# Seven-product feed-forward groups: products copied and accumulated in PSUM, two fewer VectorE combinations, and another order of loads and steps

## The chip, the core and the metric

The kernel runs on one core of a Trainium2 chip. Its time is the device time of one execution in microseconds (us); several executions give a median. One further execution is recorded by the hardware profiler, and its rows are the trace that this document reads.

## The reference

Two layers of an encoder on 256 tokens of width 1024, all in float32. A layer is a feed-forward part, attention, and a second feed-forward part; only the feed-forward parts are touched here.

```
D_MODEL = 1024; SEQ = 256; DEPTH = 2; D_FF = 2816
def swiglu(h, w_gate, w_up, w_down):
    return (jax.nn.silu(h @ w_gate) * (h @ w_up)) @ w_down
for l in range(DEPTH):
    x = x + 0.5 * swiglu(rms_norm(x, ffn1_norm[l]), ffn1_w_gate[l], ffn1_w_up[l], ffn1_w_down[l])
    x = x + attention(rms_norm(x, mix_norm[l]))     # windowed and differential heads, w_in, w_out
    x = x + 0.5 * swiglu(rms_norm(x, ffn2_norm[l]), ffn2_w_gate[l], ffn2_w_up[l], ffn2_w_down[l])
return rms_norm(x, final_norm)
```

## The kernel before

**Precision.** TensorE multiplies in a reduced float format, fp32r. Each float32 operand is split into a high part (a ScalarE copy to fp32r, in the trace a CAST) and a low part (VectorE: operand minus high part). A product is three matmuls: high by high, low by high, high by low.

**Weights.** All weights come in pieces of 1 MB, 128 partitions by 4 by 512 float32, listed in `specs` in the order of use. SP loads a piece into one of six buffers (`raw`, `N_RAW = 6`). Each piece is split in two halves of 128 x 1024; a half becomes a high and a low tile from a pool of 28 (`s4`). A buffer is free for the next load when the second half of what it holds has been split. `ahead` interleaves three streams in program order, each as far ahead of use as it may go: loads (`dma`, up to `AHEAD = 10` steps ahead, as long as a buffer is free), preparations (`prep`) and splits (`split`, up to `look` half pieces ahead of the half in use). ScalarE, VectorE and GpSimd keep the written order in the feed-forward parts (`Kept`), TensorE always.

**A feed-forward part.** The 2816 columns are five groups of 512 and one of 256. The products for gate and up of a group, then SiLU and product (`h`, 256 tokens by 512), are followed by the down product of the group before it, in two halves of 512 output columns (`down(g, 0)`, `down(g, 1)`), which accumulate over all groups in four PSUM banks (`accs`). `h` is turned by TensorE (`turn`: eight 128x128 transposes, then a high copy on ScalarE and a low part on VectorE).

**Seven products.** Groups 2 to 4 of the first feed-forward part and groups 1 to 4 of the other three (`SEVEN`), 15 in all, compute gate and up together in the Strassen-Winograd form: of the two halves of the tokens (columns of the turned x) and the two halves of K there are seven products of 128x512x512 instead of eight. With a, d the upper and lower K half of gate and b, c those of up, the weights of the products are a, d, c, a+b, b+c, a+b+c and a+b+c+d. Each is formed in the raw buffers before it is split:

- b+c and a+b are formed by accumulating DMAs that GpSimd issues (`gather`: `pool.dma_start(raws[to], w[k], accum_op=ALU.add)`). The first is issued when b has landed (`behind=`); the second when a has been split (`prep` of the step behind a).
- a+b+c and a+b+c+d are formed by VectorE in the buffer of a (`plus`, two adds of 128x1024 each). So the buffer of a holds in turn a, a+b, a+b+c and a+b+c+d.

Order of the steps before: a, b+c, d, c, down half 0, a+b, a+b+c, a+b+c+d, down half 1. In the first seven-group that is group 1, b+c stands behind c. The x-side sums (`make_sums`) are made once for a part.

**PSUM.** Eight banks of 128 x 512 float32, all under the tag `ps`. In a seven-group the four combinations of products (u1, g1, u0 in two steps, ...) are formed on VectorE from PSUM and from copies that ScalarE makes (`m1`, `m7`).

Of the kernel before, what the change touches and what calls it, by code (L numbers as in the profile page):

```python
# [12 lines left out]
ALU = mybir.AluOpType  # L13
# [21 lines left out]
def trunk(ctx: ExitStack, tc: tile.TileContext, x, n1, g1, u1, d1, nm, w_in, sink,  # L35
# [35 lines left out]
    def bank():  # L71
        return ps.tile([P, 512], F32, tag="ps", bufs=8, name=nm_("ps"))

# [18 lines left out]
    class Step:  # L92
        def __init__(self, kn, n, moves, key=None, prep=None, src=None, free=None, behind=None):
            self.kn, self.n, self.moves, self.prep = kn, n, moves, prep
# [164 lines left out]
    for l in range(DEPTH):  # L259
        def ffn_specs(wg, wu, wd, sevens):  # L260
# [3 lines left out]
            for g in range(1, NGRP):  # L264
                downs = [down(g - 1, h) for h in range(2)]
                if g in sevens:
                    specs.extend(seven(wg[l], wu[l], g * 512, downs, g == 1))
                else:
                    specs.extend(plain(w[l], g * 512, 512, k0, 4) for w in (wg, wu) for k0 in (0, 4))
                    specs.extend(downs)  # L270
            for k0 in (0, 4):
# [34 lines left out]
    class Norm:  # L306
# [42 lines left out]
        def make_sums(self):  # L349
# [18 lines left out]

            s1 = add(b1, t1, ALU.subtract)
            s2 = add(s1, t0, ALU.add)  # L370
            yield
# [158 lines left out]
    def tokens(accs, xs, w, k0, ks=range(4), first=0, last=KC - 1, order=None, cols=slice(None), h=None):  # L530

        for k, t in (order or [(k, t) for k in ks for t in range(2)]):
            kk = k0 + k
            hi, lo = w.part(k, cols, h)
            xv = xs[kk // 2][:, kk % 2]
            xh, xl = xv[:, t * P:(t + 1) * P], xv[:, S + t * P:S + (t + 1) * P]
            pe.matmul(accs[t], lhsT=xh, rhs=hi, start=kk == first, stop=False)
# [22 lines left out]
    def first_groups(norm, ws):  # L560

        sls = [halves(bank()) for _ in ws]
        for k in range(0, KC, 2):
# [38 lines left out]
    def ffn(norm, aside=None, before=None, final=False, sevens=SEVEN[1]):  # L602
# [33 lines left out]

        def by_seven(h, g):


            flat = lambda: tmp().rearrange("p a n -> p (a n)")  # L640

            def put(o, x, y, op):
                dve.tensor_tensor(o, x, y, op=op)
                return o

            late, run = g == max(sevens), 1 in sevens
            m1, m7 = flat(), flat()


            if g > 1:  # L650
                g0 = prod(norm.quarter(0, 0), weights())
                act.copy(m1, g0)
                p7 = prod(norm.summed(3), weights(1, True))
                act.copy(m7, p7)
                hT = turn(h, 2)
                prod(norm.quarter(0, 1), weights(), g0)
                p3 = prod(norm.summed(2), weights())
                if not run:
                    g0 = silu(flat(), g0, 0)
                down(hT, g - 1, 0, weights())  # L660
                if run:
                    g0 = silu(flat(), g0, 0)
            else:
                p1 = prod(norm.quarter(0, 0), weights(1, True))
                hT = turn(h, (0,))
                w = weights(1, True)
                act.copy(m1, p1)
                p2 = prod(norm.quarter(0, 1), w)
                hT += turn(h, (1,))
                g0 = put(flat(), p2, m1, ALU.add)  # L670
                down(hT, 0, 0, weights())
                silu(g0, g0, 0)
                p3 = prod(norm.summed(2), weights())
                p7 = prod(norm.summed(3), weights(1, True))
                act.copy(m7, p7)
            h = blk(F32)
            p5 = prod(norm.summed(0), weights())
            prod(norm.summed(1), weights(look[0] - 5 if late else run, late or run), p7)
            u1 = put(m1, p7, m1, ALU.subtract)
            p4 = prod(norm.quarter(1, 1), weights(look[0] - 4 if late else 3 * run, late or run))  # L680
            g1 = put(flat(), p4, u1, ALU.subtract)
            w = weights(look[0] - 3 if late else 2 * run)
            silu(g1, g1, 1)
            put(u1, u1, p5, ALU.subtract)
            u0 = put(m7, u1, m7, ALU.subtract)
            put(u0, u0, p3, ALU.add)
            if run and g == max(sevens) - 1:
                ahead(2 * at["use"] - 2 + look[0] - 1)
            up(h, u0, g0, 0)
            up(h, u1, g1, 1)  # L690
            down(hT, g - 1, 1, w)
            return h
# [12 lines left out]

        accs = [[bank(), bank()] for _ in range(2)]

        def down(hT, g, h, w):
            tokens(accs[h], [None] * (2 * g) + hT, w, 4 * g, last=(FC - 1, G4 - 1) if final and h else FC - 1)


        gs, us = [bank(), bank()], [bank(), bank()]
        if before is None:
# [33 lines left out]
        for n in range(1, NGRP):  # L747
            if n in sevens:
                look[0] = IN_FFN + min(sevens) - n if before is not take_x else IN_MIX - (n == NGRP - 1)
                h = by_seven(h, n)  # L750
                continue
            sums = norm.make_sums()
            gs = [bank(), bank()]
            tokens(gs, norm.xs, weights(), 0)
            hT = turn(h, 2)
            norm.copies()
# [4 lines left out]
            us = [bank(), bank()]  # L761
# [4 lines left out]
            for hh in range(2):  # L766
                down(hT, n - 1, hh, weights())
                if hh == 0:
                    next(sums, None)

        gu = [bank(), bank()]
        tokens(gu, norm.xs, weights(), 0)
# [55 lines left out]
    def mix(l, norm, nxt_norm):  # L828
# [23 lines left out]

        def scores(q, kb, dist, slopes, init, den):

            sl = [bank(), bank()]
            for t in range(2):
# [19 lines left out]
        def soft_b(h, q):  # L876

            den = den_b[:, h]
            e, _ = scores(q, kbs["b", h], distB, [slopeB[h]] * 2, [3e38] * 4, den)
            d2 = den.rearrange("p (t a) -> p a t", a=2)  # L880
# [56 lines left out]
        vB = tp.tile([P, 2, 512], F32, tag="v", bufs=1, name=nm_("v"))  # L937
        vsl = [bank() for _ in range(2)]
        for k0 in (0, 4):
# [44 lines left out]
        oT = [blk() for _ in range(4)]  # L984
        rsl, osl = [[bank() for _ in range(2)] for _ in range(2)]
        for t in range(2):
# [175 lines left out]
```

## Time and profile before

| | |
|---|---|
| Median of 3 executions | 918.29 us (917.4 to 919.19) |
| Profiled execution | 917.39 us, its span 915.6 us |
| Matmul on TensorE (PE) | 904.5 us busy, 99% |
| VectorE (DVE) | 792.5 us, 87% |
| ScalarE (ACT) | 589.8 us, 64% |
| GpSimd (POOL) | 66.4 us, 7% |
| Granted TensorE clock | 0.999 |

A timeline row has the start, the length, the engine, the line of the kernel, the operation with what it writes and reads, its count, and in brackets how long the engine had been idle and what ended that. Nearly all rows name L50, the helper that issues for the kept engines, so groups are told apart by their tiles: `raw` weights, `w` split weights, `s` a tile of the `s4` pool (split x or h), `q` and `v` the x-side sums, `tmp` scratch, `ps` PSUM. A DMA's row on an engine is its issue; from issue to landing is given apart. "a <-b" names as releaser the last semaphore that the profile sees.

### The profile page before, as it was taken

To read this page: it belongs to the slowest core of one execution; us is meant where nothing else is said; L and a number is where in the kernel's file an instruction comes from. 1 tells how busy PE (TensorE), PEld (TensorE's weight loads), DVE (VectorE), ACT (ScalarE), POOL (GpSimd) and SP (SyncE) were. 2 spreads that over 40 slices of the span, in tenths; PEclk is the share of its full clock that TensorE was granted. 3 is DMA by queue.
4 is the path that set the end of the run, shared out by engine and by line. 5 is a ranking of instruction groups with operands and counts; after the bars stand their busy time and mean duration, and the time that the engine had idled before them with its cause. 6 is when DMAs were issued, how large, how long until landed. Compare 5 with 4: busy or idle time off the path is not lost.

```text
span 915.6 us, 12544 instructions
## 1 busy us (share of the span) xinstructions
PE 904.5 (99%) x4696; PEld 763.7 (83%) x4696; DVE 792.5 (87%) x1096; ACT 589.8 (64%) x917; POOL 66.4 (7%) x83
## 2 busy tenths in 40 slices
PE   8999999999999999999999999999999999999997
PEld 6888888899888888888888888888998888888886
DVE  6768999959975999999789999997797689999994
ACT  7836676557865766576486666665677496666561
POOL 0400100000010100100010010000001010010011
PEclk9999999999999999999999999999999999999999
DMA  9996898828436698898767998887463467998831
GB/s 339 355 238 173 265 297 268 238 93 240 136 108 189 158 280 248 257 273 275 258 164 201 276 285 217 265 293 219 116 230 98 139 153 201 275 289 230 259 132 47
DMA packets 114061, 200.87 MB, mean 219 GB/s; under 512 B 3662, under 2 KB 31376, under 8 KB 114000
## 3 DMA queue, kind: packets, MB, share of 16 engines
q1 hardware_dynamic: 96528, 166.74, 54.5%
q0 software_dynamic: 16096, 31.75, 19.3%
q10 hardware_dynamic: 1376, 1.57, 0.5%
q8 instruction: 37, 0.61, 0.3%
q14 instruction: 24, 0.20, 0.1%
HBM read 199.00 MB, written 1.05 MB: 218 GB/s over the span
## 4 chain that ended last, share of the span: by engine, by line
PE 98%; issue 1%; DMA 0%; ACT 0%; DVE 0%; POOLq 0%; POOL 0%; ACTq 0%
PE ps L50 98%; DMA xk<-in_x_dram 0%; ACT w L50 0%; DVE s L50 0%; DVE xk L50 0%; ACT tmp L50 0%; ACT L50 0%; POOLq L1157 0%; POOL rf L50 0%; ACTq L50 0%; DVE tot L50 0%; DVE tmp L50 0%
## 5 line engine op out<-in xcount | busy, mean ns | idle before, releaser
L50 PE MATMUL ps<-w,s 128*128 128x512 f32 (+1 forms) x2574 | 600.2, 391 | 0.5 <-ACT tmp L50 0.5
L50 PEld LDWEIGHTS ps<-w,s 128*128 128x128 f32 x2574 | 477.6, 188 | 100.3 <-ACT tmp L50 2.3
L50 DVE TENSOR_TENSOR w<-raw,w 128x1024 fp32r<-128x1024 f32 (+1 forms) x458 | 482.1, 1101 | 37.8 <-ACT w L50 36.6
L50 ACT CAST w<-raw 128x1024 fp32r<-128x1024 f32 (+1 forms) x458 | 409.8, 954 | 122.6 <-DVE raw L50 78.4
L50 PE MATMUL ps<-w,q 128*128 128x512 f32 x540 | 127.3, 389 | 0.0
L50 PEld LDWEIGHTS ps<-w,q 128*128 128x128 f32 x540 | 101.4, 188 | 21.0
L50 PE MATMUL ps<-s,w 128*128 128x256 f32 x672 | 83.1, 284 | 0.0
L50 PEld LDWEIGHTS ps<-s,w 128*128 128x128 f32 x672 | 81.5, 192 | 0.5
L50 POOL DMA_DIRECT2D raw<-in_ffn_w_up_dram x30 | 38.9, 1296 | 472.8 <-DVE w L50 240.8
L50 DVE TENSOR_TENSOR raw<-raw,raw 128x1024 f32<-128x1024 f32 x60 | 70.7, 1219 | 0.0
L50 ACT ACTIVATE s<-ps,gcol 128x256 fp32r<-128x256 f32 (+1 forms) x80 | 31.7, 480 | 43.7 <-PE ps L50 42.1
L50 ACT CAST s<-ps 128x512 fp32r<-128x512 f32 x44 | 24.3, 594 | 29.9 <-PE ps L50 29.9
L50 PE MATMUL ps<-w,v 128*128 128x512 f32 x180 | 43.3, 389 | 0.0
L50 ACT COPY tmp<-ps 128x512 f32<-128x512 f32 x34 | 19.9, 585 | 36.2 <-PE ps L50 34.0
L50 ACT ACTIVATE s<-s,negm 128x256 f32<-128x256 f32 x64 | 31.9, 500 | 14.8 <-DVE negm L50 14.8
L50 PE MATMUL ps<-ident,s 128*128 128x128 f32 x304 | 39.7, 273 | 0.0
L50 PEld LDWEIGHTS ps<-w,v 128*128 128x128 f32 x180 | 33.8, 188 | 7.0
L50 PEld LDWEIGHTS ps<-ident,s 128*128 128x128 f32 x304 | 35.1, 140 | 5.1 <-issue 0.8
L50 DVE TENSOR_TENSOR s<-ps,s 128x512 fp32r<-128x512 f32 x44 | 28.7, 686 | 9.1 <-ACT s L50 9.1
L50 DVE SCALAR_TENSOR_TENSOR s<-ps,gcol,s 128x256 fp32r<-128x256 f32 x48 | 20.3, 478 | 11.6 <-ACT s L50 11.5
L50 DVE TENSOR_TENSOR tmp<-ps,tmp 128x512 f32<-128x512 f32 x37 | 25.4, 686 | 2.7 <-PE ps L50 2.1
L50 DVE TENSOR_TENSOR xk<-xk,ps 128x512 f32<-128x512 f32 (+1 forms) x25 | 14.1, 598 | 14.9 <-PE ps L50 14.9
(106 smaller groups left out, 404.7 us busy)
## 6 DMA issues: line engine op xcount, KB each, us to landing
raw<-in_ffn_w_down_dram SPq DMA_DIRECT2D x44, 1024.0 KB, 8.9
raw<-in_ffn_w_gate_dram SPq DMA_DIRECT2D x39, 1024.0 KB, 6.4
raw<-in_ffn_w_up_dram SPq DMA_DIRECT2D x39, 1024.0 KB, 5.7
raw<-in_ffn_w_up_dram POOLq DMA_DIRECT2D x30, 1024.0 KB, 12.3
raw<-in_w_in_dram SPq DMA_DIRECT2D x14, 1024.0 KB, 6.1
raw<-in_ffn_w_gate_dram SPq DMA_DIRECT2D x8, 512.0 KB, 6.2
raw<-in_ffn_w_up_dram SPq DMA_DIRECT2D x8, 512.0 KB, 7.2
raw<-in_w_in_dram SPq DMA_DIRECT2D x8, 512.0 KB, 5.3
```

The costliest lines, as they stand in the source:

```text
L50: ins = issue(*a, **k)
```

## The change

What it does, in a seven-group:

- PSUM becomes six single banks and one pair of banks (`xy`). ScalarE writes the negated first product p1 into both banks of the pair; the products of c and of b+c accumulate onto these. The product p5 of a+b is copied by ScalarE into the bank of p1, where p4 (weights a+b+c+d) accumulates; the product of a+b+c accumulates on p5 itself. VectorE then needs three combinations, two fewer. The x-side sums change sign to fit.
- The add for a+b+c, and for a+b+c+d, is one VectorE instruction of 128x2048 instead of two of 128x1024.
- `h` is turned by token halves (`turn_one(h, t)`: four transposes, copy, low part, once for each half) instead of by column halves.
- Order of the steps: a, down half 1 deferred from the group before (`below`, of the h two groups back), d, c, down half 0, a+b, b+c, a+b+c, a+b+c+d. So b is loaded last, behind the down piece, and each down half 1 is used in the next group. In a first seven-group without an earlier one in its part it is a, d, down half 0, c, and then the same.
- The four accumulators are taken when first used, the look-ahead (`lead`) is 8, 8, 7, 7 half pieces instead of 8, 7, 6, 5 in parts with four such groups, and the preparation of a+b+c may go one step earlier (`early=1`).

The number of matmuls, of loads and of accumulating DMAs stays as it was. VectorE has 1098 instructions before and 1038 after, ScalarE 855 and 837, counted in the program.

```diff
-        return ps.tile([P, 512], F32, tag="ps", bufs=8, name=nm_("ps"))
+        return ps.tile([P, 512], F32, tag="ps", bufs=6, name=nm_("ps"))
+    def pair():
+        return ps.tile([P, 2, 512], F32, tag="xy", bufs=1, name=nm_("xy"))
...
-    def seven(wg, wu, c0, downs, first):
+    def seven(wg, wu, c0, below, down):
...
-                for h in (0, 2):
-                    x_, t_ = [raws[i][:, h:h + 2] for i in (x, to)]
-                    dve.tensor_tensor(t_, t_, x_, op=ALU.add)
+                dve.tensor_tensor(raws[to], raws[to], raws[x], op=ALU.add)
...
-        bc = Step(4, 512, load(b), key=b, behind=gather(c, b))
-        rest = [Step(4, 512, load(d), key=d, free=[]), Step(4, 512, load(c), key=c, free=[]), downs[0]]
-        steps = [rest[0], rest[2], rest[1], bc] if first else [bc] + rest
+        steps = [Step(4, 512, load(d), key=d, free=[]), Step(4, 512, load(c), key=c, free=[])]
+        steps = [below] + steps + [down] if below is not None else [steps[0], down, steps[1]]
         steps[0].prep = lambda: issue(gather(b, a), 1)
         return [Step(4, 512, load(a), key=a, free=[])] + steps + [
                 Step(4, 512, None, src=a, free=[]),
-                Step(4, 512, None, prep=plus(c, a), src=a, free=[c]),
-                Step(4, 512, None, prep=plus(d, a), src=a, free=[a, d]),
-                downs[1]]
+                Step(4, 512, load(b), key=b, behind=gather(c, b)),
+                Step(4, 512, None, prep=plus(c, a), src=a, free=[c], early=1),
+                Step(4, 512, None, prep=plus(d, a), src=a, free=[a, d])]
...
-                    (specs[at["prep"]].prep is None or at["split"] >= 2 * at["prep"]):
+                    (specs[at["prep"]].prep is None or at["split"] >= 2 * (at["prep"] - specs[at["prep"]].early)):
...
+        def turn_one(h, t):
+            sl = bank()
+            for k in range(4):
+                pe.transpose(sl[:, k * P:(k + 1) * P], h[:, t, k * P:(k + 1) * P], ident)
+            hb = blk()
+            act.copy(hb[:, 0], sl)
+            dve.tensor_tensor(hb[:, 1], sl, f(hb[:, 0]), op=ALU.subtract)
+            return hb
...
+        def by_sevens(h, groups, old):
...
+            xy = pair()
+            for g in groups:
+                start, late = old is None, g == groups[-1]
+                look[0] = lead(g)
+                p1 = prod(norm.quarter(0, 0), weights(start, start))
+                act.activation(xy, p1.unsqueeze(1).to_broadcast([P, 2, 512]), AF.Copy, scale=-1.0)
+                if start:
+                    g0 = flat()
+                    act.copy(g0, p1)
+                new = [turn_one(h, 0)]
+                if start:
+                    p2 = prod(norm.quarter(0, 1), weights())
+                    new.append(turn_one(h, 1))
+                    dve.tensor_tensor(g0, p2, g0, op=ALU.add)
+                    below(by_token(new), g - 1, 0, weights(), [(k, t) for t in range(2) for k in range(4)])
+                    silu(g0, g0, 0)
+                    prod(norm.summed(2), weights(), xy[:, 1])
+                else:
+                    below(old, g - 2, 1, weights())
+                    new.append(turn_one(h, 1))
+                    prod(norm.quarter(0, 1), weights(), p1)
+                    prod(norm.summed(2), weights(), xy[:, 1])
+                    below(by_token(new), g - 1, 0, weights())
+                    g0 = silu(flat(), p1, 0)
+                old = by_token(new)
+                p5 = prod(norm.summed(0), weights())
+                act.copy(p1, p5)
+                prod(norm.summed(3), weights(), xy[:, 0])
+                prod(norm.summed(1), weights(look[0] - 5 if late else 1, True), p5)
+                e = flat()
+                act.copy(e, p5)
+                u1, u0 = flat(), flat()
+                dve.tensor_tensor(u0, xy[:, 1], e, op=ALU.add)
+                dve.tensor_tensor(u1, xy[:, 0], e, op=ALU.add)
+                h = blk(F32)
+                up(h, u0, g0, 0)
+                p4 = prod(norm.quarter(1, 1), weights(look[0] - 4 if late else 3, True), p1)
+                g1 = flat()
+                dve.tensor_tensor(g1, p4, u1, op=ALU.subtract)
...
+                silu(g1, g1, 1)
+                up(h, u1, g1, 1)
+            below(old, groups[-1] - 1, 1, w)
             return h
...
-        accs = [[bank(), bank()] for _ in range(2)]
+        accs = []
+        def lead(n):
+            return IN_FFN - (n - min(sevens)) // 2 if before is not take_x else IN_MIX - (n == NGRP - 1)
```

The other edits take the pair of banks in place of two single ones in the plain groups and in the attention part, or fit callers to the new functions.

More of the change, by code (lines that the diff above doesn't have):

```diff
@@ L266, in ffn_specs @@
                 if g in sevens:
-                    specs.extend(seven(wg[l], wu[l], g * 512, downs, g == 1))
+                    specs.extend(seven(wg[l], wu[l], g * 512, down(g - 2, 1) if g > 1 else None, downs[0]))
+                    if g == max(sevens):
+                        specs.append(downs[1])
                 else:
                     specs.extend(plain(w[l], g * 512, 512, k0, 4) for w in (wg, wu) for k0 in (0, 4))
-                    specs.extend(downs)
+                    specs.extend(downs[:1] if g + 1 == min(sevens) else downs)
             for k0 in (0, 4):
@@ L560, in first_groups @@
     def first_groups(norm, ws):
-        sls = [halves(bank()) for _ in ws]
+        both = pair()
+        sls = [halves(both[:, i]) for i in range(2)]
         for k in range(0, KC, 2):
@@ L635, in prod @@
             return acc
-        def by_seven(h, g):
-            flat = lambda: tmp().rearrange("p a n -> p (a n)")
[L642 to L691, printed above, removed]
@@ new lines, in below @@
+        def below(of, g, h, w, order=None):
+            while len(accs) <= h:
+                accs.append([bank(), bank()])
+            tokens(accs[h], of, w, 4 * g, last=(FC - 1, G4 - 1) if final and h else FC - 1, order=order)
+        def by_sevens(h, groups, old):
+            flat = lambda: tmp().rearrange("p a n -> p (a n)")
+            xy = pair()
[15 more added lines that the diff above has]
+                    prod(norm.summed(2), weights(), xy[:, 1])
+                else:
+                    below(old, g - 2, 1, weights())
[19 more added lines that the diff above has]
+                dve.tensor_tensor(g1, p4, u1, op=ALU.subtract)
+                if late:
+                    w = weights(look[0] - 3)
+                else:
+                    ahead(2 * at["use"] + look[0] - 2)
+                silu(g1, g1, 1)
+                up(h, u1, g1, 1)
+            below(old, groups[-1] - 1, 1, w)
@@ L704, in turn, with both @@
             return out_
-        accs = [[bank(), bank()] for _ in range(2)]
+        accs = []
+        def lead(n):
+            return IN_FFN - (n - min(sevens)) // 2 if before is not take_x else IN_MIX - (n == NGRP - 1)
         def down(hT, g, h, w):
+            while len(accs) <= h:
+                accs.append([bank(), bank()])
             tokens(accs[h], [None] * (2 * g) + hT, w, 4 * g, last=(FC - 1, G4 - 1) if final and h else FC - 1)
-        gs, us = [bank(), bank()], [bank(), bank()]
+        def both():
+            p = pair()
+            return [p[:, t] for t in range(2)]
+        gs, us = [bank(), bank()], both()
         if before is None:
@@ L748, in ffn @@
             if n in sevens:
-                look[0] = IN_FFN + min(sevens) - n if before is not take_x else IN_MIX - (n == NGRP - 1)
-                h = by_seven(h, n)
+                if n == min(sevens):
+                    h = by_sevens(h, sevens, by_chunk(hT) if n > 1 else None)
                 continue
@@ L760, in ffn @@
             next(sums, None)
-            us = [bank(), bank()]
+            us = both()
             for k0 in (0, 4):
@@ L765, in ffn @@
             h = hidden(g, us)
-            for hh in range(2):
+            for hh in range(1 if n + 1 == min(sevens) else 2):
                 down(hT, n - 1, hh, weights())
@@ L851, in q_finish, with scores @@
             return [q[:, 0], q[:, 1]]
-        def scores(q, kb, dist, slopes, init, den):
-            sl = [bank(), bank()]
+        def scores(q, kb, dist, slopes, init, den, wide=False):
+            both = pair() if wide else None
+            sl = [both[:, i] if wide else bank() for i in range(2)]
             for t in range(2):
@@ L937, in mix @@
         vB = tp.tile([P, 2, 512], F32, tag="v", bufs=1, name=nm_("v"))
-        vsl = [bank() for _ in range(2)]
+        both = pair()
+        vsl = [both[:, t] for t in range(2)]
         for k0 in (0, 4):
@@ L984, in mix @@
         oT = [blk() for _ in range(4)]
-        rsl, osl = [[bank() for _ in range(2)] for _ in range(2)]
+        rsl, both = [bank() for _ in range(2)], pair()
+        osl = [both[:, t] for t in range(2)]
         for t in range(2):
```

24 lines of the change are left out of this document (15 added, 9 removed).

## The prediction

> **What bounds the kernel now.** I read the page's busy shares first, then the chain that ended last, then the costliest groups, and then the timelines of the engines over the first two seven-groups of the second FFN.
>
> ```profile
> span 915.6 us, 12544 instructions
> PE 904.5 (99%) x4696; PEld 763.7 (83%) x4696; DVE 792.5 (87%) x1096; ACT 589.8 (64%) x917; POOL 66.4 (7%) x83
> 31.04 873.94 PE ps L50 x4547
> ```
>
> The third line is one link of the chain of waits: from 31.04 us on the chain never leaves TensorE for 873.94 us. So a faster VectorE cannot shorten this run by itself; only fewer or denser matmuls could, and the change keeps all of them in number and shape. The question is whether TensorE stays fed.
>
> The pace of one seven-group stands in TensorE's timeline, by the transposes that open each group, and in the busy times of the stretches between:
>
> ```profile
> 343.59 1.03 PE L50 MATMUL ps<-ident,s 128*128 128x128 f32 x8
> ...
> 347.23 2.88 PE L50 MATMUL ps<-w,q 128*128 128x512 f32 x12
> 349.95 5.60 PE L50 MATMUL ps<-w,s 128*128 128x512 f32 x24
> ...
> 374.44 1.03 PE L50 MATMUL ps<-ident,s 128*128 128x128 f32 x8
> 405.25 1.04 PE L50 MATMUL ps<-ident,s 128*128 128x128 f32 x8
> 320.00:350.80 30.80, 30.80 (x141) 25.59 (x140) 29.59 (x31) 20.65 (x25) 2.57 (x2) 1.00 0.90 248
> ```
>
> A group lasts 30.8 us (405.25 - 374.44), and one product of 12 matmuls 2.72 (349.95 - 347.23). The last row is a stretch: start and end, length, then busy time of PE, PEld, DVE, ACT, POOL, then clock, DMA share, GB/s. VectorE is busy 29.6 of 30.8 us, so it is the second limit, close behind.
>
> **VectorE and ScalarE work.** The change drops two 128x512 combinations per group, 30 in all:
>
> ```profile
> L50 DVE TENSOR_TENSOR tmp<-tmp,ps 128x512 f32<-128x512 f32 x30 | 20.5, 684 | 0.5
> L50 DVE TENSOR_TENSOR raw<-raw,raw 128x1024 f32<-128x1024 f32 x60 | 70.7, 1219 | 0.0
> L50 ACT COPY tmp<-ps 128x512 f32<-128x512 f32 x34 | 19.9, 585 | 36.2 <-PE ps L50 34.0 <-DVE w L50 2.1
> L50 ACT ACTIVATE tmp<-ps,r 128x512 f32<-128x512 f32 x22 | 14.6, 690 | 0.0
> ```
>
> That is about 30 x 0.68 = 20 us off VectorE, 1.4 us a group, none of it on the chain. The 60 adds of 128x1024 become 30 of 128x2048. No such size is in the trace: two of the old ones take 2 x 1219 ns, a single one is a floor of 1.22; I take 2.35, what a pair takes in a row below. ScalarE gains one 128x1024 negated copy into PSUM (nearest rows: between one 585 ns copy and two 690 ns activations, 1.38; I take 1.2) and one 128x512 bank-to-bank copy (585 to 690 ns) per group, and loses 12 copies: about 15 x 1.8 - 12 x 0.6 = 20 us more, in 20.7 of 30.8 us busy, so off the chain where inputs are in time. The transposes in two fours instead of one eight cost TensorE nothing (360 ns from 309.98 to 310.34 below, twice, against 790 for eight).
>
> **The order is what costs.** Before, a group's pieces were loaded as a, b, d, c, down; now b comes last, after the down piece. Six raw buffers are all in use then, and the buffer that b of the next group gets is that of a, which is free only when a+b+c+d, built in it, has had its second half split. So a loop closes across groups: last split of a+b+c+d, load of b, accumulating transfer b+c, accumulating transfer a+b (queued behind it on GpSimd, which waits for b's landing, although a+b needs nothing of b's buffer), then the splits and adds up to the next a+b+c+d. TensorE's 30.8 us are not in it. In the kernel before, b took the buffer of b+c, much earlier, and no such loop binds. Its links are in these rows (SP's, GpSimd's, ScalarE's, VectorE's and TensorE's timeline, then DMA):
>
> ```profile
> 314.57 0.37 SPq L153 DMA_DIRECT2D raw<-in_ffn_w_up_dram  x1
> 320.19 1.28 POOL L50 DMA_DIRECT2D raw<-in_ffn_w_up_dram  x1 [17.16 <-DMA raw<-in_ffn_w_up_dram]
> 332.44 1.28 POOL L50 DMA_DIRECT2D raw<-in_ffn_w_up_dram  x1 [10.97 <-DVE w L50]
> 309.98 0.60 PE L50 MATMUL ps<-ident,s 128*128 128x128 f32 x4
> 310.34 3.00 PE L50 MATMUL ps<-w,s 128*128 128x512 f32 x12
> 313.82 0.59 ACT L50 CAST s<-ps 128x512 fp32r<-128x512 f32 x1 [0.23 <-PE ps L50]
> 314.30 2.00 ACT L50 CAST w<-raw 128x1024 fp32r<-128x1024 f32 x2
> 314.46 0.68 DVE L50 TENSOR_TENSOR s<-ps,s 128x512 fp32r<-128x512 f32 x1
> 315.66 2.35 DVE L50 TENSOR_TENSOR w<-raw,w 128x1024 fp32r<-128x1024 f32 x2
> 317.93 2.35 DVE L50 TENSOR_TENSOR raw<-raw,raw 128x1024 f32<-128x1024 f32 x2
> 324.89 2.42 DVE L50 TENSOR_TENSOR w<-raw,w 128x1024 fp32r<-128x1024 f32 x2
> raw<-in_ffn_w_up_dram POOLq DMA_DIRECT2D x30, 1024.0 KB, 12.3
> DMA to landing us min/median/max: 8.4/12.3/15.0
> q0 software_dynamic: 16096, 31.75, 19.3%
> ```
>
> 1. Load of b to issue of b+c: 320.19 - 314.57 = 5.6 us, GpSimd waiting for the landing.
> 2. The pair. One accumulating transfer lands 8.4 to 15.0 us after issue, median 12.3, among loads. In the loop SP's queue stands nearly dry, since no raw buffer is free, so I take the middle of least and median, 10.4. The second shares the queue: 19.3% of 915.6 us for 30 is 5.9 us of all 16 engines each. Pair: 10.4 + 5.9 = 16.3; ends 8.4 + 1.3 = 9.7 (the second wholly beside the first, an issue of 1.3 us later) and 15.0 + 5.9 = 20.9.
> 3. Splits and adds. Before, from the first cast of a+b at 314.30 to the end of the last split of a+b+c+d at 324.89 + 2.42 = 327.31: 13.0 us. After, the two b+c splits (2 x 1.13, half of a 2.35 pair less overlap) and one split of a turned half (0.6) come to lie in it: 15.9.
> 4. Hand-overs between engines and to SP: 0.5.
>
> Loop: 5.6 + 16.3 + 15.9 + 0.5 = 38.3 us; ends 31.7 and 42.9. Against 30.8 TensorE loses 7.5 us a turn. FFNs with four seven-groups have 3 turns, the first, with three, has 2: 3 x 3 + 2 = 11 turns, 82.5 us.
>
> **The first group of each four.** There the splits of a+b and b+c and the first 128x2048 add come ahead, in ScalarE's and VectorE's kept order, of the second turned half of h. Before, that half was ready at 314.46 + 0.68 = 315.1 and the down product followed. After, it waits for a+b (its first cast was at 314.30 before) and then some 4 x 1.13 + 2.35 us: about 321, while TensorE wants it at 317 (p1 ends at 309.98, transposes 0.36, p2 2.75, transposes, four chunks of token 0, 2.7, and a little). A stall of 4 us, three times, of which the loop behind takes part over. What counts is how late the last product, p4, ends: before, two products and one down product ahead of the transposes at 343.59, so at 343.59 - 4 x 2.72 = 332.7. After, the last split ends at 327.3 + 2.6 (b+c's two splits and hand-overs) = 329.9, and p4 some 6.3 later (ScalarE's copy of p5 stands behind a cast and a SiLU, 0.9, then two products), at 336.2: 3.5 us late in each of three FFNs. In the first FFN the first seven-group is no such start; the same count gives 0.9. Together 11.4 us.
>
> Sum: 917.4 (the profiled execution: span 915.6 and 1.8 around it) + 82.5 + 11.4 = 1011.3; the median is 0.9 above the profiled run, so 1012. Each us of the loop is worth 11.
>
> **A rule against it.** The row for accumulating transfers has 12.3 us, at best 8.4. The Trainium skill, "DMA: Bandwidth & Descriptors", section "Anatomy of one DMA — SWDGE (gpsimd) path", fits a transfer from GpSimd as 2.0 us plus bytes over 436 GB/s, which would be an estimate of 4.4 us for this megabyte. By that rule the pair would be done in about 7 us and the loop would fall under 30.8; the trace disagrees with it for transfers that add.
>
> **Rivals.**
> - Short transfers: with SP dry, the pair overlaps and lands within 9.7 us. The loop is 31.7, 0.9 over TensorE: 11 x 0.9 + 11.4 = 21 us, 939. For it: 8.4 occurs. Against it: the two share 16 engines that one holds for 5.9 us. 0.11.
> - The loop stays under 30.8 altogether and only the first groups stall: 917.4 + 11.4 = 929 (0.04). This is what the rule just named would make.
> - Longer: loads of a, c, d and down crowd into the same stretch and the pair takes its upper end or more: from 42.9 on, 917.4 + 11 x 12.1 + 11.4 = 1062 and up. 0.08.
> - Faster: b's load starts early after all, since ScalarE and VectorE, with 1.4 us a group less to do, run ahead of TensorE and finish a+b+c+d well before it is used. It decides if the loop stays under 30.8 and a+b lands some 4 us earlier in the first groups. The gain is small even then, since there is little to win: in the row below TensorE's weight loads waited 2.3, 1.2 and 0.2 us for ScalarE and VectorE in the whole run, 3.7 in all. 917.4 - 3.7 = 914. Chance 0.03.
>
> ```profile
> L50 PEld LDWEIGHTS ps<-w,s 128*128 128x128 f32 x2574 | 477.6, 188 | 100.3 <-ACT tmp L50 2.3 <-DVE w L50 1.2 <-DVE s L50 0.2
> ```
>
> - The change does nothing: the same products with all waits hidden, 918. Chance 0.02.
>
> **How the numbers follow.** The likeliest case, a loop of 34 to 42.9 us, has 0.72: 964 to 1062, at 38.3 us 1012. To hold 8 in 10 the range takes in half of the short transfers and the longer case's start: 945 to 1065. Faster or slower here means by over 0.2%, 1.8 us, about what a measurement can tell: faster 0.03, same 0.02, slower 0.95.
>
> **What would show it.** Right: TensorE's busy share falls to about 90%; ScalarE's casts wait for the accumulating transfers 7 or more us a group, as the groups' row or the waits show; the transposes of successive groups lie about 38 us apart; GpSimd issues its two transfers back to back in each group; the chain runs in turn through the load of b, GpSimd and VectorE. In the first group of an FFN TensorE waits about 4 us for VectorE's s. Wrong: groups still 30.8 us apart, or a+b landing before TensorE has finished the down products; then the loop's sum is wrong, the pair first of all, since it is the least known term.

## The result

The changed kernel takes 1020.46 us (median of 5 executions, 1018.54 to 1021.12) against 918.29 for the one before: a ratio of 1.111 (95% interval 1.109 to 1.113), 102 us slower. The forecast was 1012 us, from 945 to 1065. The page of the changed kernel, its first line, the busy shares and the chain that ended last:

```profile
span 1019.3 us, 12444 instructions
PE 941.9 (92%) x4696; PEld 780.5 (77%) x4696; DVE 772.6 (76%) x1036; ACT 602.1 (59%) x935; POOL 63.7 (6%) x83
PE 44%; DMA 23%; DVE 20%; ACT 7%; issue 6%; POOL 0%; ACTq 0%; POOLq 0%; DVEq 0%
```

The chain had one link of 873.94 us on TensorE before; now TensorE carries 44% of it. VectorE has 20 us less to do, as counted, and the kernel gained nothing by it. The chain's longest pieces (start, length, what) over two turns in the second feed-forward part:

```profile
382.53 5.07 DMA raw<-in_ffn_w_up_dram
388.91 14.90 DMA raw<-in_ffn_w_up_dram
406.71 2.35 DVE w L50 x2
409.06 2.20 DVE raw L50
412.42 1.11 issue
414.78 2.30 DVE raw L50
419.78 1.24 DVE w L50
421.03 5.01 DMA raw<-in_ffn_w_up_dram
427.33 15.61 DMA raw<-in_ffn_w_up_dram
```

These are the steps of the forecast, in its order: the load of b (5.07), the accumulating transfer of a+b that started 0.75 us after that of b+c (14.90), the splits and the two adds, the last split, and the next load of b at 421.03, 38.5 us after 382.53. TensorE is not in it. The whole chain has the load of b eleven times, once for each turn that the forecast counted. GpSimd's timeline:

```profile
350.85 2.59 POOL L50 DMA_DIRECT2D raw<-in_ffn_w_up_dram  x2 [32.39 <-DMA raw<-in_ffn_w_up_dram]
388.16 2.59 POOL L50 DMA_DIRECT2D raw<-in_ffn_w_up_dram  x2 [34.72 <-DMA raw<-in_ffn_w_up_dram]
426.58 2.59 POOL L50 DMA_DIRECT2D raw<-in_ffn_w_up_dram  x2 [35.82 <-DMA raw<-in_ffn_w_up_dram]
```

Two issues stand in one row, 37.3 and 38.4 us apart, each pair behind b's landing; before, in this part, they were single rows 12 to 22 us apart. TensorE's timeline of the same stretch:

```profile
325.77 3.00 PE L50 MATMUL ps<-w,s 128*128 128x512 f32 x12
336.08 4.37 PE L50 MATMUL ps<-w,s 128*128 128x512 f32 x11 [3.64 <-DVE s L50]
384.06 4.61 PE L50 MATMUL ps<-w,q 128*128 128x512 f32 x12 [3.92 <-ACT ps L50]
421.23 4.61 PE L50 MATMUL ps<-w,q 128*128 128x512 f32 x12 [4.11 <-ACT ps L50]
```

The first row is the second product of the first seven-group, 15.4 us later than before (310.34). Of that the first feed-forward part has lost 14.9: the transposes that follow it stand at 198.35, before at 183.46. The second is the stall in the first group of a part. The others are products of a+b+c that wait for ScalarE's copy of p5.

### The profile page after: what moved, and what is told of

Read it like the earlier page. It is cut to its first block, busy times and chain, and to the rows that moved or that the text cites. A ratio compares the mean times of both kernels' runs of the same rounds, so it can differ in the third digit from the quotient of the medians.

```text
span 1019.3 us, 12444 instructions
## 1 busy us (share of the span) xinstructions
PE 941.9 (92%) x4696; PEld 780.5 (77%) x4696; DVE 772.6 (76%) x1036; ACT 602.1 (59%) x935; POOL 63.7 (6%) x83
## 4 chain that ended last, share of the span: by engine, by line
PE 44%; DMA 23%; DVE 20%; ACT 7%; issue 6%; POOL 0%; ACTq 0%; POOLq 0%; DVEq 0%
PE ps L50 31%; DMA raw<-in_ffn_w_up_dram 22%; PE xy L50 12%; DVE w L50 10%; DVE raw L50 7%; ACT w L50 4%; ACT s L50 2%; DVE s L50 2%; ACT tmp L50 1%; DVE tmp L50 1%; DMA xk<-in_x_dram 0%; ACT xy L50 0%; DVE q L50 0%; POOL raw L50 0%; ACT ps L50 0%
## 5 line engine op out<-in xcount | busy, mean ns | idle before, releaser
L50 PE MATMUL ps<-w,s 128*128 128x512 f32 (+1 forms) x2046 | 494.6, 396 | 18.5 <-DVE s L50 15.3
L50 PEld LDWEIGHTS ps<-w,s 128*128 128x128 f32 x2046 | 382.5, 191 | 104.9 <-DVE s L50 19.4
L50 PE MATMUL ps<-w,q 128*128 128x512 f32 x360 | 107.6, 458 | 45.3 <-ACT ps L50 45.3
L50 PE MATMUL xy<-w,s 128*128 128x512 f32 x528 | 125.2, 391 | 0.0
L50 PEld LDWEIGHTS xy<-w,s 128*128 128x128 f32 x528 | 98.4, 188 | 20.3
L50 DVE TENSOR_TENSOR raw<-raw,raw 128x2048 f32<-128x2048 f32 x30 | 68.7, 2288 | 0.5
L50 PE MATMUL ps<-s,w 128*128 128x256 f32 x480 | 59.2, 284 | 0.0
L50 PEld LDWEIGHTS ps<-s,w 128*128 128x128 f32 x480 | 58.1, 192 | 0.4
L50 ACT ACTIVATE s<-ps,gcol 128x256 fp32r<-128x256 f32 (+1 forms) x80 | 31.7, 479 | 43.9 <-PE ps L50 42.3
L50 PE MATMUL xy<-w,v 128*128 128x512 f32 x180 | 43.5, 390 | 0.6 <-DVE w L50 0.6
L50 PE MATMUL xy<-w,q 128*128 128x512 f32 x180 | 43.8, 392 | 0.0
L50 ACT CAST s<-ps 128x512 fp32r<-128x512 f32 x44 | 25.3, 587 | 30.9 <-PE ps L50 30.9
L50 DVE TENSOR_TENSOR tmp<-xy,tmp 128x512 f32<-128x512 f32 x30 | 19.3, 687 | 29.2 <-ACT tmp L50 29.2
L50 PEld LDWEIGHTS xy<-w,q 128*128 128x128 f32 x180 | 34.6, 192 | 7.4
```

Of the source, the lines that this page charges most:

```text
L50: ins = issue(*a, **k)
```

## Experiments

Ratios are to the kernel before, run beside each; 95% intervals in brackets.

**One transfer out of the loop.** The changed kernel with b+c's transfer made a preparation of its own step, so that GpSimd issues a+b first:

```diff
-                Step(4, 512, load(b), key=b, behind=gather(c, b)),
+                Step(4, 512, load(b), key=b, prep=lambda: issue(gather(c, b), 2)),
```

> The changed kernel, with one thing moved: GpSimd issues a+b ahead of b+c, so that a+b no longer stands behind b's landing. Theory (the loop over b's buffer, with the pair of accumulating transfers in it): one of the two transfers leaves the loop. The loop becomes the load 5.6, b+c 10 to 12, the chain from b+c's first split to the last split of a+b+c+d 13.3, and hand-overs 0.5: 29.4 to 31.4, about TensorE's 30.8. The transposes of successive groups come 31 to 32 us apart and the time falls to 925 to 945 us. Rival (splits and adds are slow of themselves, or loads crowd): the groups stay above 36 us apart and the time above 985.

969.4 us, 1.056 [1.054, 1.059]: 51 us back, about as much still lost, and above the range expected. GpSimd's timeline of this run:

```profile
376.92 1.28 POOL L50 DMA_DIRECT2D raw<-in_ffn_w_up_dram  x1 [1.48 <-DMA raw<-in_ffn_w_up_dram]
407.89 1.28 POOL L50 DMA_DIRECT2D raw<-in_ffn_w_up_dram  x1 [29.70 <-DVE w L50]
410.66 1.28 POOL L50 DMA_DIRECT2D raw<-in_ffn_w_up_dram  x1 [1.49 <-DMA raw<-in_ffn_w_up_dram]
```

and its chain, with the load of b and the transfer that follows:

```profile
405.22 5.16 DMA raw<-in_ffn_w_up_dram
410.66 13.68 DMA raw<-in_ffn_w_up_dram
```

The loop fell to 33.7 us (410.66 - 376.92). The expectation had given b+c 10 to 12 us; it took 13.7, with a+b's transfer issued 2.8 us ahead of it (407.89) on the same queue. So taking a+b out of the wait takes out its latency, and not its share of the engines.

The edit also did more than was meant. In the first group of the second part the two transfers are now issued back to back (305.44), the second lands 15.9 us after its start, and TensorE waits twice for a turned half of h that stands behind the casts of that piece:

```profile
324.72 0.79 PE L50 MATMUL ps<-w,s 128*128 128x512 f32 x1 [4.40 <-ACT s L50]
328.49 4.92 PE L50 MATMUL ps<-w,s 128*128 128x512 f32 x11 [2.98 <-DVE s L50]
```

That is 7.4 us where the changed kernel waits 3.64, and the chain passes through the second wait. The first group lasts 35.8 us from its transposes to the next (313.75 to 349.58), where the same products take 25.7 in the run without the copy below (311.72 to 337.39). The later transposes come 31.7 and 32.4 us apart (381.27, 413.71), much as expected. So in this part more of what is still lost lies in the first group than in the loop.

**b in its old place.** The changed kernel's products, with b+c loaded and used behind the deferred down piece:

```diff
+        bc = Step(4, 512, load(b), key=b, behind=gather(c, b))
+        steps = [below, bc] + steps + [down] if below is not None else [steps[0], down, steps[1], bc]
...
-                Step(4, 512, load(b), key=b, behind=gather(c, b)),
-                Step(4, 512, None, prep=plus(c, a), src=a, free=[c], early=1),
+                Step(4, 512, None, prep=plus(c, a), src=a, free=[c]),
...
                     new.append(turn_one(h, 1))
+                    prod(norm.summed(3), weights(), xy[:, 0])
...
                 act.copy(p1, p5)
-                prod(norm.summed(3), weights(), xy[:, 0])
```

> The changed kernel with the old place of b: b+c is loaded, split and used behind the deferred down piece (in a first seven-group behind c), as in the kernel before, while the products still accumulate in PSUM on copies. Theory: no loop binds, since b takes a buffer that a down piece leaves much earlier; groups 30.8 us apart; what is left is the first groups' wait for the second turned half, a part of it, since one cast of a+b still lies ahead of it: 918 to 932 us. Rival (the PSUM copies on ScalarE cost it): ScalarE's copy of p5 holds p4 up by 2 us or more in each of 15 groups, 950 or more.

1005.5 us, 1.095 [1.090, 1.100]. The rival was nearer. The loop over b is gone (but for the first pair GpSimd's issues are single again, 11 to 26 us apart in a part, and the chain holds no load and no transfer of these weights), and groups are still 36.4 us apart. TensorE's, ScalarE's and VectorE's timelines of this run:

```profile
363.52 0.60 PE L50 MATMUL ps<-ident,s 128*128 128x128 f32 x4
383.95 2.88 PE L50 MATMUL ps<-w,q 128*128 128x512 f32 x12
390.03 4.60 PE L50 MATMUL ps<-w,q 128*128 128x512 f32 x12 [3.20 <-ACT ps L50]
399.96 0.60 PE L50 MATMUL ps<-ident,s 128*128 128x128 f32 x4
383.14 3.90 ACT L50 CAST w<-raw 128x1024 fp32r<-128x1024 f32 x4 [3.88 <-DVE raw L50]
389.40 0.58 ACT L50 COPY ps<-ps 128x512 f32<-128x512 f32 x1
380.73 2.29 DVE L50 TENSOR_TENSOR raw<-raw,raw 128x2048 f32<-128x2048 f32 x1
```

p5 ends by 386.8 (its row starts at 383.95 and has 2.88), but the copy of it, which the next product accumulates on, starts at 389.40: in ScalarE's kept order it stands behind casts that wait 3.88 us for VectorE's add of d. TensorE waits, the next h is later, its turned half stands ahead of a+b's casts, and the circle closes again, now through TensorE and ScalarE's order. The chain runs that way, and the gaps of 1.1 us behind the wide adds lie in it too. So a second loop lay under the first one.

**The order alone.** The kernel before, with its combinations and narrow adds, and b last:

```diff
-        steps = [rest[0], rest[2], rest[1], bc] if first else [bc] + rest
+        steps = [rest[0], rest[2], rest[1]] if first else rest
...
                 Step(4, 512, None, src=a, free=[]),
+                Step(4, 512, load(b), key=b, behind=gather(c, b)),
...
             p5 = prod(norm.summed(0), weights())
+            p7 = prod(norm.summed(3), weights())
+            act.copy(m7, p7)
```

> The kernel before, with one thing changed: b is loaded last and b+c is used behind a+b; old combinations on VectorE, old turning of h, adds of 128x1024, down halves in the old places. Theory: the order alone makes the loop; it has the same load, pair and splits: groups 36 to 40 us apart and 990 to 1030 us. Rival (the cost comes from the PSUM copies, the wide adds or the turning): within 2% of the kernel before, below 937.

985.4 us, 1.073 [1.068, 1.078], a little under the range. The order alone makes about two thirds of the loss. Groups are 34.4 and 37.0 us apart (transposes at 354.78, 389.18 and 426.17). But this is not the loop over b alone. Loads and transfers of these weights have 10% of this run's chain, 22% of the changed kernel's, and from 340 to 425 us the chain holds none of them. It goes through VectorE's splits and adds, ScalarE's copy of p7 (the product of b+c) and TensorE, which waits for that copy:

```profile
375.44 3.02 PE L50 MATMUL ps<-w,q 128*128 128x512 f32 x12 [2.12 <-ACT tmp L50]
409.63 5.49 PE L50 MATMUL ps<-w,q 128*128 128x512 f32 x12 [3.00 <-ACT tmp L50]
```

Moving b last also moved p7 directly ahead of the product that accumulates on it. So this run prices the order, and not the loop over b by itself.

**The first group's stall.** The changed kernel with both halves of h turned ahead of the second product in a first group:

```diff
-                new = [turn_one(h, 0)]
+                new = [turn_one(h, t) for t in range(2 if start else 1)]
...
                     p2 = prod(norm.quarter(0, 1), weights())
-                    new.append(turn_one(h, 1))
```

> The changed kernel with the second half of h turned ahead of the second product in a first seven-group, so that its copy and low part no longer stand behind the splits of a+b and b+c. Theory (the stall of 3.6 us in each first group is covered by the loop that follows, which does not go through TensorE): the stall is gone from the trace and the time is the same, 1017 to 1021 us. Rival (it adds to the loop): 3 x 3.6 = 11 us less, 1009.

1016.9 us, 1.108 [1.106, 1.111], an interval that overlaps the changed kernel's, and near the 1017 to 1021 expected, not the 1009 of a sum. The wait of 3.64 us is gone from TensorE's timeline, which has another of 2.80 for the copy of p5 later in the same group. So a stall in front of a loop that doesn't pass through TensorE cost next to nothing here.

**The copy's place, the loop over b left in.** The look-ahead is cut at the down product and at p5, and the next step catches up:

```diff
-                    below(by_token(new), g - 1, 0, weights())
+                    below(by_token(new), g - 1, 0, weights(max(look[0] - 7, 0), True))
...
-                p5 = prod(norm.summed(0), weights())
+                p5 = prod(norm.summed(0), weights(look[0] - 5, True))
```

> The changed kernel with the look-ahead held shorter at the down product and at p5 of the groups behind the first, so that in ScalarE's order the copy of p5 into p1's bank stands ahead of the casts of a+b+c+d and of the next a. The run with b in its old place still had groups 36 us apart: there TensorE waited for this copy, and the copy for six casts behind the add of d. First theory (a second loop through ScalarE's order lies just under the loop over b's buffer): here the loop over b stays, so groups stay 37 to 39 us apart, and only the last group of each part gains 2 to 3 us: 1005 to 1016 us. Rival (the copy's place is what costs, and the loop over b is not what binds): groups under 34 us, below 970.

977.6 us, 1.063 [1.059, 1.066], outside what the first theory allowed. But the edit did more than was meant: GpSimd's order turned round by itself in the later pairs of the last three parts, probably since b's load is emitted later. Its timeline:

```profile
390.22 1.28 POOL L50 DMA_DIRECT2D raw<-in_ffn_w_up_dram  x1 [33.42 <-DVE w L50]
393.06 1.28 POOL L50 DMA_DIRECT2D raw<-in_ffn_w_up_dram  x1 [1.56 <-DMA raw<-in_ffn_w_up_dram]
423.29 1.28 POOL L50 DMA_DIRECT2D raw<-in_ffn_w_up_dram  x1 [28.94 <-DVE w L50]
426.16 1.28 POOL L50 DMA_DIRECT2D raw<-in_ffn_w_up_dram  x1 [1.59 <-DMA raw<-in_ffn_w_up_dram]
```

The first of each pair waits for VectorE's w, a's splits, so it is a+b; b+c comes 2.9 us behind. So this run can't part the two loops; it is in the main the first experiment again, and lands near it (969.4).

**All three moved.** a+b first, both halves turned early, shorter look-ahead:

> The changed kernel with three things moved at once: a+b ahead of b+c on GpSimd, the second half of h turned early in first groups, and the shorter look-ahead around the copy of p5. Theory of two loops: both are cut to about TensorE's 30.8 or just over, since b+c alone still waits for b's load: groups 30.8 to 32 us apart, 920 to 940 us. Rival (something else than these binds): as with the swap alone, 960 or more.

959.5 us, 1.044 [1.042, 1.047]; the theory's range is missed by 20 us, and the rival's figure of 960 or more by a hair. Groups are 31.7 and 32.1 us apart (345.81, 377.47, 409.56), and in some groups the chain still passes the load of b and the transfer behind it (370.44, 5.08 us, and 376.06, 13.77 us).

**c in b's place.** b+c goes back behind the deferred down piece, and c, which needs no accumulating transfer, goes where b was; its product then lies between p5 and that of a+b+c. With both halves turned early and the shorter look-ahead:

```diff
+        bc = Step(4, 512, load(b), key=b, behind=gather(c, b))
+        steps = [below, bc, steps[0], down] if below is not None else [steps[0], down, bc]
...
-                Step(4, 512, load(b), key=b, behind=gather(c, b)),
+                Step(4, 512, load(c), key=c, free=[]),
...
-                prod(norm.summed(3), weights(), xy[:, 0])
+                prod(norm.summed(2), weights(), xy[:, 1])
```

> The changed kernel with b in the old place, behind the deferred down piece, and c in b's: c needs no accumulating transfer of its own and its product lies between p5 and the product of a+b+c, where it hides the copy of p5. With the second half of h turned early in first groups and the shorter look-ahead. Theory of two loops: neither is left: groups 30.8 to 31.2 us apart and 916 to 926 us. Rival (the PSUM copies cost in themselves): 940 or more.

936.2 us, 1.018 [1.017, 1.020]: 84 of the 102 us are back. It lies between the theory's range and the rival's.

**Not adding.** The changed kernel with b+c's transfer writing c over b, so that b is left out of that sum:

```diff
-                pool.dma_start(raws[to], w[k], accum_op=ALU.add)
+                pool.dma_start(raws[to], w[k], **({} if k is c else dict(accum_op=ALU.add)))
```

> The changed kernel with the transfer that makes b+c not adding: it writes c over b, so the product of b+c is left out of the sum (its output is another). If adding is what makes a transfer from GpSimd long, the first of the pair lands in 5 to 6 us after issue instead of 8 to 10, the pair takes 11 to 13 us instead of 15 to 16, and the loop falls until the second loop of 36 us binds: 990 to 1000 us. If GpSimd's path is what is long, the landing stays at 8 us or more and the time within 1% of 1020.

984.7 us in one execution, a little under the range expected. GpSimd's transfers of weights, issue to landing, in the changed kernel and then in this one (half of them adding):

```profile
DMA to landing us min/median/max: 8.2/11.3/16.8
```

```profile
DMA to landing us min/median/max: 5.8/9.1/13.6
```

The least is 5.8, about what a load from SP takes (median 5.4 in the page of the changed kernel), where none came under 8.2 before the edit. The two kinds part cleanly: the first transfer of a pair, which no longer adds, lands 5.8 to 8.0 us after issue, and in the changed kernel, where it adds, 8.2 to 11.7. So the adding lengthens a transfer, and the loop with it: in the second part the pairs are issued 36.4 and 35.6 us apart instead of 37.3 and 38.4.

**The copy's place and the copy itself, no loop over b.** First the kernel with c in b's place and the look-ahead of the changed kernel; then the same without `act.copy(p1, p5)`, with p4 in a bank of its own, so that p5's share is left out of one combination:

> As the run with c in b's place, but with the look-ahead of the changed kernel, so that ScalarE's copy of p5 stands again behind the casts of a+b+c+d. No loop over b is in it. Theory (the copy's place in ScalarE's order makes a second loop: turned half of h, a+b, two adds, casts, copy, then the products up to the next turned half): groups 33 to 35 us apart, TensorE waits for ScalarE's ps, 942 to 968 us. Rival (the copy's place does not matter once b comes early): as with the shorter look-ahead, 936 us within 0.5%.

> As the run before it in this call (c in b's place, look-ahead of the changed kernel, second half of h turned early), with the copy of p5 into p1's bank left out, so that a+b+c accumulates on p5 at once and p4 starts in a bank of its own: p5's share is missing from one combination. Theory: without the copy nothing on TensorE waits for ScalarE's casts and the second loop is gone: groups 30.8 to 31.5 us apart, 916 to 926 us. Rival (VectorE, 29 of 30.8 us busy, or the turned halves limit it whatever the copy): 930 or more.

939.6 us, 1.022 [1.019, 1.025], and 932.3, 1.015 [1.012, 1.018]. The place of the copy is worth about 3 us, the copy some 7: the rival held both times. With a product of 2.72 us between p5 and the product of a+b+c, little is left of the second loop. In the run without the copy two groups of the second part are 30.9 us apart (371.08, 401.97). Most of the 13.5 us still lost there are waits of TensorE for VectorE's part of a turned half (us in all, times, longest):

```profile
PE ps L50 <- DVE s L50: 8.6, 8, 2.5
```

**The wide adds alone**, in the kernel before:

```diff
-                for h in (0, 2):
-                    x_, t_ = [raws[i][:, h:h + 2] for i in (x, to)]
-                    dve.tensor_tensor(t_, t_, x_, op=ALU.add)
+                dve.tensor_tensor(raws[to], raws[to], raws[x], op=ALU.add)
```

> The kernel before with the wide adds alone: 30 of 128x2048 in place of 60 of 128x1024. Theory (only the order costs): VectorE's work is the same, the first cast behind an add waits 1.1 us longer, covered by the half us to some us by which the splits are early: 917 to 921 us. Rival (the wide add makes splits late, since they are early by little): TensorE waits about 1 us in most of 15 groups, 925 to 935 us.

943.6 us, 1.028 [1.026, 1.030]: 25 us for an edit that the forecast had at nothing. VectorE and ScalarE of this run, then of the kernel before:

```profile
359.32 2.29 DVE L50 TENSOR_TENSOR raw<-raw,raw 128x2048 f32<-128x2048 f32 x1
362.73 2.36 DVE L50 TENSOR_TENSOR w<-raw,w 128x1024 fp32r<-128x1024 f32 x2 [1.12 <-ACT w L50]
361.65 2.00 ACT L50 CAST w<-raw 128x1024 fp32r<-128x1024 f32 x2 [4.30 <-DVE raw L50]
```

```profile
350.39 2.36 DVE L50 TENSOR_TENSOR raw<-raw,raw 128x1024 f32<-128x1024 f32 x2
352.74 2.36 DVE L50 TENSOR_TENSOR w<-raw,w 128x1024 fp32r<-128x1024 f32 x2
351.65 2.19 ACT L50 CAST w<-raw 128x1024 fp32r<-128x1024 f32 x2 [3.46 <-DVE raw L50]
```

Before, ScalarE casts the first half (351.65) beside the second add, and VectorE goes on without a gap (352.74). With one add the cast starts when all of it is done (361.65) and VectorE stands for 1.12 us, twice a group: 2.2 us on an engine with 1.2 us to spare. Groups come 32.0 and 32.7 us apart.

**All of it.** c in b's place, shorter look-ahead, early turning, and narrow adds:

> The kernel with c in b's place, the shorter look-ahead and the second half turned early, with its adds in halves of 128x1024 again. The wide adds alone cost the kernel before 25 us: ScalarE's first cast behind an add waits for the whole of it, and VectorE then stands idle for about 1.1 us, twice a group, on 29 of 30.8 us busy. Theory (the wide adds are what is left of the loss): VectorE's chain of a group falls from 32 or 33 to about 30.5 us, groups 30.8 to 31.2 us apart, 916 to 924 us. Rival (the rest comes from the turned halves and the copy, in ScalarE's order): 930 to 937 us.

933.9 us, 1.016 [1.014, 1.018]: the theory falls, only 2 us came. Its timelines, ScalarE, VectorE, TensorE:

```profile
391.84 0.57 ACT L50 COPY ps<-ps 128x512 f32<-128x512 f32 x1 [5.29 <-PE ps L50]
393.40 5.77 DVE L50 TENSOR_TENSOR w<-raw,w 128x1024 fp32r<-128x1024 f32 x5 [2.93 <-ACT w L50]
409.01 0.69 DVE L50 TENSOR_TENSOR s<-ps,s 128x512 fp32r<-128x512 f32 x1
409.76 0.66 PE L50 MATMUL ps<-ident,s 128*128 128x128 f32 x4 [1.20 <-DVE s L50]
```

With the copy early in the order it is ScalarE that waits, 5.29 us for p5; the casts of a+b+c+d stand behind it, and VectorE is idle 2.93. From there it works without a gap to the turned half at 409.01, and TensorE waits 1.20 us for that before its transposes. So a circle of 32.3 us (transposes at 377.44 and 409.76) remains, by this trace through the copy's wait. Such waits for the turned half make up most of the last 15 us:

```profile
PE ps L50 <- DVE s L50: 11.7, 11, 1.8
```

Why VectorE is late there is read from this trace and not shown. Narrow adds with the copy left out would show it; that was not run. No version was faster than the kernel before.

## Why the prediction was right, point by point

- **What bounds it.** Right: TensorE was packed, and the 20 us taken from VectorE bought nothing.
- **The loop, 38.3 us.** The starts of b's loads in the chain are 37.8 to 39.5 us apart within a part, 38.8 in the mean. The terms of the turn of 38.5 us shown above: load to issue 388.16 - 382.53 = 5.6, as said; the pair 388.91 + 14.90 - 388.16 = 15.7, against 16.3 (16.4 in the next turn); splits and adds with hand-overs, from a+b's landing (388.91 + 14.90 = 403.8) to the next load of b at 421.03, 17.2 against 16.4. In the last lie two gaps in which VectorE waits for ScalarE's first cast behind a wide add, 1.11 us at 412.42 in the chain and 1.19 us ahead of this row:

```profile
418.26 1.22 DVE L50 TENSOR_TENSOR w<-raw,w 128x1024 fp32r<-128x1024 f32 x1 [1.19 <-ACT w L50]
```

  The forecast had not seen them: its term came from rows with narrow adds. They are more than the excess, so the rest of the term was put too high, and that the sum came so near is in part luck.
- **That it is this loop.** Shown in part: the chain passes through it in every turn, taking one transfer from it gave 51 us, making one not add 36. Moving b last in the old kernel costs 67, but by its chain in part through another circle. The loop was not the only one: with b in its old place it is gone, and only 15 us come back. The forecast said what would bind, not what lay under it, and its price of 11 us for each us of the loop ends where the next circle binds, here at some 36 us.
- **The first groups, 3.5 us each, and the stall covered by the loop.** The stall was 3.64, 4 forecast; taking it away gave 3.6 us in all, inside the noise, where three stalls would have added to 11. The load of b that waits for the first group's last split starts at 344.72; less the 15.4 us of a later start that is 329.3, forecast 329.9. The first part lost 14.9, forecast 15 + 0.9.
- **The wide add, at 2.35 us "what a pair takes".** Wrong in kind: its length was right (2288 ns), its price isn't its length but the cast that no longer overlaps. Alone, in the kernel before, it costs 25 us. The changed kernel with narrow adds was not run, so what it costs there is open.
- **The copies on ScalarE, "off the chain where inputs are in time".** Inputs were not in time. The forecast counted the copy's delay once per part, at p4's end; TensorE waited for it 11 times, 45.3 us in the groups' row. In the changed kernel these waits lie mostly beside the loop over b. ScalarE's work grew by 12 us (589.8 to 602.1), not 20; by the pages it has 18 instructions more (917 and 935), where the count under "The change" has 18 fewer.

```profile
L50 PE MATMUL ps<-w,q 128*128 128x512 f32 x360 | 107.6, 458 | 45.3 <-ACT ps L50 45.3
```

- **The 8 us missed.** By the transposes behind them the four parts lost 14.9, 28.2, 29.2 and 29.9 us, where the forecast has 15.9 and three times 26; so the miss lies in the last three. A loop longer by half a us, eleven times, is some 5 of it. Another part is the clock after the last wait of a part, where the products stand on the chain. TensorE's row and the busy times by stretch (the clock behind POOL's column):

```profile
460.36 5.49 PE L50 MATMUL ps<-w,q 128*128 128x512 f32 x12 [4.12 <-ACT ps L50]
460.00:466.00 6.00, 5.64 (x13) 4.47 (x14) 3.63 (x4) 2.34 (x4) 0.00 (x0) 0.50 0.85 303
466.00:476.00 10.00, 10.00 (x44) 8.18 (x43) 8.93 (x11) 7.68 (x9) 0.00 (x0) 0.98 0.51 164
```

  Twelve matmuls took 5.49 us instead of 2.88 at a granted clock of 0.50. At the end of a part nothing covers this: there the twelve took 4.37, 5.49, 4.61 and 5.27 us in the four parts, 8.2 us more than four times 2.88. The two together are more than the miss; what offsets them was not traced.
- **The rule on GpSimd's transfers.** The estimate of 4.4 us by the Trainium skill ("DMA: Bandwidth & Descriptors", "Anatomy of one DMA — SWDGE (gpsimd) path") was not reached: 8.2 us at the least where the transfer adds, 5.8 where it doesn't. The forecast by the trace's rows held.

## What to carry to other kernels

When a reordering moves a load to the end of a cycle, write down which buffer it gets, what frees that buffer, and what the loaded piece feeds: if this comes back to the same buffer, the sum round the circle is a lower bound on the cycle, whatever the busiest engine does. Work it out for every circle, those through an engine's fixed order too: under the 38 us one here lay others of some 36 and 32 (the runs with b in its old place and with all of it), so removing one gave less than its excess. And two half instructions can be worth more than one whole where another engine starts on the first half.

## What the hardware showed

- An accumulating transfer of 1 MB from GpSimd landed in 8.2 us at the least, one that overwrites in 5.8. Of two adding ones issued back to back in the changed kernel, the second landed 12.7 to 16.8 us after its start.
- After a wait of 4.12 us TensorE's granted clock was 0.50 for the next 6 us or so (460 to 466); after other waits of the changed kernel it recovered sooner (twelve matmuls in 4.61 us behind 3.92 and 4.11). The Trainium skill ("TensorE: Matmul & The Clock Gate", "Part 1: The HAM clock gate") has the clock halve after an idle window of about 3.4 us. The waits of 3.92 to 4.12 agree with it, but in the run with b in its old place twelve matmuls took 4.60 us after a wait of 3.20 only (390.03), so here a shorter one was enough.
- One VectorE add of 128x2048 took 2288 ns, a pair of 128x1024 2.36 us: the wide form saves 0.1 us.
